# Gated DeltaNet: where e^g meets the queries, in the feature-major q or in the token rows of q S

## The chip, the cores and the metric

The kernel runs on one core of a Trainium2 chip. The metric is the device time of one execution in microseconds; times are medians over several executions. One further execution was recorded by the hardware profiler, and all lines of the profile are from it. TensorE (PE, its weight loads PEld), VectorE (DVE), ScalarE (ACT), GpSimd (POOL) and SyncE (SP, which issues most DMAs here) each work off a queue of their own, in order.

## The reference, cut to what matters

Two layers of a diffusion trunk over 128 context tokens and 256 latent tokens of 1024 features. Layer 0 runs HGRN2 and gated DeltaNet side by side between one input and one output projection; layer 1 is neighbourhood attention; each layer ends with a squared-ReLU MLP. DeltaNet has four heads of 128, goes over the tokens forward and backward, and is defined chunk by chunk:

```python
g = jnp.cumsum(glog.reshape(b, h, n, CHUNK), axis=-1)
...
attn = jnp.where(tri, jnp.einsum('bhntd,bhnsd->bhnts', q, k) * L, 0.0)
qg = q * jnp.exp(g)[..., None]
...
v_new = u_n - jnp.einsum('bhtd,bhdv->bhtv', w_n, s)
o_n = jnp.einsum('bhtd,bhdv->bhtv', qg_n, s) + jnp.einsum('bhts,bhsv->bhtv', attn_n, v_new)
s = jnp.exp(gl_n)[..., None, None] * s + jnp.einsum('bhsd,bhsv->bhdv', kdec_n, v_new)
...
o_b = _rmsnorm(ob_f + ob_b, gn_b) * jax.nn.silu(_heads(g_b, H_B).astype(f32))
```

The output of a token is the part that comes from the past, (q e^g) S, plus the part from its own chunk, attn v_new, summed over both directions and normalized. e^g is one number for each token, head and direction.

## The kernel before, in words

The 384 tokens are three tiles of 128: tile 0 is the context, tiles 1 and 2 the latents. A chunk is a whole tile here, so each tile and direction has one step of the recurrence (`gdn_step`). Tile 0 starts from no state; for tiles 1 and 2 there are the given states S0 and one state S that each direction hands on. fp32 operands of the large projections are split into two reduced-precision parts and take three matmuls (L646 to L648 for features in rows, L673 to L675 for tokens in rows); DeltaNet's own products are plain fp32, each of which the trace records as two rows.

`gdn_steps` is a generator that gives one step of DeltaNet at each "d" in the order string `STEPS`; the other letters are HGRN2's steps, the adaptive-norm products, the blocks of the input projection, the four gate blocks "g" and HGRN2's part of the output ("m"). What is written in this order is then put into each engine's queue by the framework's scheduler, which works with a simulation of its own, so that a change at one place can move instructions of other steps. `ORDER` fixes a few places by hand: the matmuls of gate 2 are held behind the last product of `gdn_out(2, ...)`, those of gate 3 behind `gdn_out(1, ...)`.

At the end of the mixer the steps around the change are these. `gdn_attn` makes k·q for all tiles (L1012) and DVE multiplies it with the decay that is already in `AT_` (L1014). `gdn_eps` squares q on ACT (L1022) and sums the squares with one-column matmuls against ones (L1024), for the epsilon of the output's norm; DVE finishes it (L1026). `gdn_qg`, for one tile and direction, makes e^g spread over features: DVE multiplies a triangle with the upper and lower part of log g (L1035), two fp32r matmuls with ones sum over tokens (L1037), ACT takes the exponential out of the bank (L1039), and POOL multiplies it into q, which lies features by tokens (L1040). `gdn_out` sums attention times new values (L1197) and this q times S (L1200) for both directions in one PSUM bank; `out_norm` squares it by head on ACT, with the sums as a second output (L1251), DVE adds epsilon (L1253), POOL takes the root (L526), and DVE scales (L1257). Tile 0 has no past and so no L1200.

Then `gdn_step` for tile 0: k S and the solved new values (L1165), the evacuation of w (L1168 on ACT), k transposed (L1173, evacuated by L1175), its product with the weighted new values (L1180) and the new state (L1183, L1186). The gate blocks run the sigmoid on ACT (L1240) and a product on DVE (L1241). `mix_out` transposes each normalized tile (L1266), multiplies the gate in and splits it (L1268 to L1271); the output projection follows.

PSUM banks rotate by tag: the tag "gd" has two banks, which each call of `ps` takes in turn, so a step that takes a bank waits until the one before the last has been read out. The pool `g2` has three buffers. L209 on ACT and L210 on DVE split a weight tile into its two parts.

Of the kernel before, what the change touches and what calls it, by code (L numbers as in the profile page):

```python
# [9 lines left out]
F32 = mybir.dt.float32  # L10
F32R = mybir.dt.float32r
AF = mybir.ActivationFunctionType
ALU = mybir.AluOpType
# [4 lines left out]
P = 128  # L18
D = 1024
KT = 8  # L20
NT = 3
# [85 lines left out]
class Trunk:  # L107
# [117 lines left out]
    def start(self):  # L225
        nc, i = self.nc, self.i
        ident, tri = self.const([P, P], "ident"), self.mixc([P, len(CONST_NAMES) - 1, P], "tri")
        self.c = {n: tri[:, k - 1] if k else ident for k, n in enumerate(CONST_NAMES)}
        nc.sync.dma_start(ident, i["consts"][:, 0, :])
        self.ones = self.mixc([P, P], "ones", F32R)  # L230
        nc.gpsimd.memset(self.ones.bitcast(F32), 1.0)
        self.c["ones"] = self.ones.bitcast(F32)
        crow = self.g2([16, P])
        nc.scalar.dma_start(crow[0:8], i["c_ctx"].rearrange("(r c) -> r c", c=P))
        nc.scalar.dma_start(crow[8:16], i["c"].rearrange("o (r c) -> (o r) c", c=P))
        brow = self.brow = self.g2([P, P])
        prow = self.prow = self.g2([76, P])
        lv = self.mixc([P, NS * 32 + 2 * P], "lv", mybir.dt.uint8)
        self.lv = {L: lv[:, k * 32:k * 32 + 32] if k < NS else lv[:, NS * 32 + (k - NS) * P:NS * 32 + (k - NS + 1) * P]
                   for k, L in enumerate(LEVELS)}  # L240
        self.eye = self.mixc([P, 32], "eye")

        def load():
            yield nc.sync.dma_start(brow[0:96], i["ada_b"].rearrange("l (r c) -> (l r) c", c=P))
            yield nc.sync.dma_start(brow[96:P], i["norm_g"].rearrange("l j (r c) -> (l j r) c", c=P))
            yield nc.sync.dma_start(prow[0:12], i["hgrn_lb"].rearrange("l (r c) -> (l r) c", c=P))
            yield nc.sync.dma_start(prow[12:13], i["gn_hgrn"])
            yield nc.sync.dma_start(prow[13:14], i["gn_gdn"])
            for j in range(2):
                yield nc.sync.dma_start(prow[14:15, j * 64:(j + 1) * 64], i["qn_na"])  # L250
                yield nc.sync.dma_start(prow[15:16, j * 64:(j + 1) * 64], i["kn_na"])
            yield nc.sync.dma_start(prow[16:76], i["gdn_conv"].rearrange("e t o (r c) -> (e t o r) c", c=P))

        def load_masks():
            nc.sync.dma_start(tri, i["consts"][:, 1:, :])
            nc.sync.dma_start(self.eye, i["levels"][:, 0:32])
            f = self.sb([P, NS * 32 + 2 * P], "lvf")
            nc.sync.dma_start(f, i["levels"][:, 32:])
            nc.gpsimd.tensor_copy(lv, f)
        self.eps = self.const([P, 5], "eps")  # L260
        nc.vector.memset(self.eps[:, 0:1], EPS)
        nc.vector.memset(self.eps[:, 1:2], EPS * P)
        nc.vector.memset(self.eps[:, 2:3], 1.0)
        nc.vector.memset(self.eps[:, 3:4], 0.0)
        nc.vector.memset(self.eps[:, 4:5], -0.5)
        pt = self.ps([P, 16], "tmp")
        nc.tensor.transpose(pt, crow, self.c["ident"][0:16, 0:16])
        cond = self.sb([P, 16], "sel")
        nc.vector.tensor_copy(cond, pt)
        sc = self.sb([P, 16], "sel")  # L270
        self.sigmoid(sc, cond)
        nc.vector.tensor_mul(sc, sc, cond)

        self.sc = self.const([P, 2 * KT + 30], "scz")
        nc.gpsimd.memset(self.sc, 0.0)

        self.sel = self.mixc([P, 4], "selc")
        pick = self.c["ident"].rearrange("p (g k c) -> p g k c", g=2, k=2)[:, :, :, 0:2]
        nc.vector.tensor_add(self.sel.rearrange("p (k v) -> p k v", k=2), pick[:, 0], pick[:, 1])
        nc.vector.tensor_copy(self.sc[:, 0:16].rearrange("p (k v) -> p k v", v=2), sc.rearrange("p (v k) -> p k v", v=2))  # L280
        return load, load_masks
# [428 lines left out]
    def evac_f(self, d, h):  # L710
        nc = self.nc

        def f(pg):
            s = self.cvt([P, NT, P])
            nc.scalar.activation(s, pg.rearrange("p (t c) -> p t c", t=NT), AF.Sigmoid)
            nc.vector.tensor_scalar(self.G[:, :, d, h], s, self.lb1[:, h:h + 1], self.lb[:, h:h + 1],
                                    op0=ALU.mult, op1=ALU.add)
# [12 lines left out]
    def hgrn_tile(self, t, Q, K):  # L730
# [5 lines left out]
        q = AT.rearrange("p h c -> p (h c)")  # L736
        G = self.G[:, t].rearrange("p d h c -> p d (h c)")
        nc.scalar.activation(K, G, AF.Identity, scale=-1.0, bias=self.eps[:, 2:3])
        ks = self.km([P, 512])
# [5 lines left out]
        for h, r, c in small:  # L745
            nc.tensor.matmul(pd[r, h], ks[:, c], q[:, c], start=True, stop=True)
        nc.vector.tensor_mul(Q[:, 0], q, G[:, 1])
        nc.vector.tensor_mul(Q[:, 1], q, G[:, 0])
        nc.vector.tensor_mul(AB, pd, self.eye.unsqueeze(1).broadcast_to([P, 4, 32]))
        tot, nt = G, 512  # L750
        yield
# [125 lines left out]
    def gates(self, h):  # L877

        nc, i = self.nc, self.i
# [31 lines left out]
        nc.vector.tensor_add(a, a, e)  # L911
        self.glog = c8("glog")
        nc.vector.tensor_mul(self.glog, a, al.unsqueeze(1).broadcast_to([P, NT, 8]))
        self.gparts = [self.mixc([P, NT, 8], n, F32R) for n in ("ghi", "glo")]
        nc.gpsimd.tensor_copy(self.gparts[0], self.glog)
        nc.gpsimd.tensor_tensor(self.gparts[1], self.glog, self.gparts[0].bitcast(F32), op=ALU.subtract)

        e3 = self.mixc([P, 3, NT, 8], "eg")
        self.eg, self.egd, self.egl = e3[:, 0], e3[:, 1], e3[:, 2]
        pe = self.ps([P, 3, NT, 8], "tmp")  # L920
# [95 lines left out]
    def gdn_eps(self):  # L1016
# [7 lines left out]
                nc.tensor.matmul(pq[:, t, h:h + 1], q2[:, t], self.c["ones"][:, 0:1], start=True, stop=True)  # L1024
        self.qe = self.mixc([P, NT, 4], "qe")
        nc.vector.tensor_scalar(self.qe, pq, EPS * EPS * P, None, op0=ALU.add)  # L1026

    def gdn_qg(self, t, d):

        nc = self.nc  # L1030
        tri = ("le", "ge")[d]
        pe = self.ps([P, 4, P], "gd")
        for n, g in enumerate(self.gparts):
            G = self.g2([P, 4, P], F32R)
            nc.vector.tensor_tensor(G, self.c[tri].unsqueeze(1).broadcast_to([P, 4, P]),  # L1035
                g[:, t, d * 4:d * 4 + 4].bitcast(F32).unsqueeze(2).broadcast_to([P, 4, P]), op=ALU.mult)
            nc.tensor.matmul(pe, self.ones, G, start=(n == 0), stop=(n == 1))  # L1037
        G = self.g2([P, 4, P])
        nc.scalar.activation(G, pe, AF.Exp)  # L1039
        nc.gpsimd.tensor_tensor(G, G, self.kq[:, t, :, 1], op=ALU.mult)  # L1040
        return G

    def gdn_solve(self):

# [142 lines left out]
                                               op0=ALU.mult, op1=ALU.add)  # L1187
        return w, S2

    def gdn_out(self, t, w, S):  # L1190
        nc = self.nc
        qg = [self.gdn_qg(t, d) for d in range(2)] if S is not None else None
        po = self.ps([P, 4, P], "gd")
        for h in range(4):
            for d in range(2):
                last = d == 1 and S is None
                self.mark["out", t] = nc.tensor.matmul(po[:, h], self.AT_[:, t, d, h], w[d][:, h], start=(d == 0), stop=last)  # L1197
            if S is not None:
                for d in range(2):
                    nc.tensor.matmul(po[:, h], qg[d][:, h], S[d][:, h], start=False, stop=(d == 1))  # L1200
        self.out_norm(1, t, po, self.vt[:, t])

    def gdn_steps(self):

        nc, i = self.nc, self.i
        for _ in zip(self.gdn_levels(0), self.gdn_levels(1)):
            yield
        S0 = self.sm4([P, 2, 4, P])
        nc.sync.dma_start(S0, i["state_gdn"][0, 0].rearrange("d h k v -> k d h v"))
        w, S = {}, {}  # L1210
        w[1, 0], S[0] = self.gdn_step(1, 0, S0[:, 0], True)
        yield
        w[2, 1], S[1] = self.gdn_step(2, 1, S0[:, 1], True)
        yield
        w[2, 0], _ = self.gdn_step(2, 0, S[0], False)
        yield
        w[1, 1], _ = self.gdn_step(1, 1, S[1], False)
        yield
        self.gdn_attn()
        self.gdn_eps()  # L1220
        yield
        self.gdn_out(2, (w[2, 0], w[2, 1]), (S[0], S0[:, 1]))
        yield
        self.gdn_out(1, (w[1, 0], w[1, 1]), (S0[:, 0], S[1]))
        yield
        for d in range(2):
            w[0, d], Sp = self.gdn_step(0, d, None, True)
            nc.sync.dma_start(self.o["state_gdn"][0, 0, d].rearrange("h k v -> k h v"), Sp)
            yield
        self.gdn_out(0, (w[0, 0], w[0, 1]), None)  # L1230
        yield
# [593 lines left out]
```

## Time and profile before

| | |
|---|---|
| median of 3 runs | 1148.52 us (1146.92 to 1149.19) |
| the profiled execution | 1152.35 us, span 1150.6 us |
| mean granted TensorE clock | 0.976 |
| busy: PE / DVE / ACT / POOL | 95% / 66% / 43% / 25% of the span |
| first L1024 to the first matmul of the output projection | 288.95 to 339.92 us |
| the first table load and exponential of L1039 | 1.28 and 0.60 us |

A row of the profile names the line of the kernel, the engine, the operation and the tiles, as out<-in. Waits are given as the engine and line that waited, "<-" the line that released it, then the total, the number and the longest. The granted clock is the share of full speed that TensorE's throttle allowed.

### The profile page before, as it was taken

The page shows a single profiled execution, that of the slowest core. Times are in us where ns is not written, and L with a number is a line of the kernel's source. Part 1 is how long each engine was busy: PE and PEld are TensorE (multiplying, and loading weights), DVE is VectorE, ACT ScalarE, POOL GpSimd, SP SyncE. Part 2 cuts the span into 40 slices and gives each one's busy share as a digit, 9 for nine tenths or more (in the row PEclk, how much of TensorE's full clock was granted, in tenths as well). Part 3 has the DMA queues.
Part 4 walks back from the last instruction along what each step waited for, and adds up shares of the span by engine and source line. Part 5 has one row for each costly group of instructions (what it writes and reads, how often), then busy time and mean ns, then how long its engine had stood idle before and what let it go on. Part 6 is the DMA issues. An engine that isn't in the chain of part 4 may idle for free.

```text
span 1150.6 us, 18007 instructions
## 1 busy us (share of the span) xinstructions
PE 1088.7 (95%) x6861; PEld 943.6 (82%) x6861; DVE 760.7 (66%) x1186; ACT 490.1 (43%) x874; POOL 289.9 (25%) x301
## 2 busy tenths in 40 slices
PE   6989978999899899999999989999988999999998
PEld 3868767988888888898889878888768889989987
DVE  3678598895356697986898565877757763333333
ACT  3465333333354553333343455555635433433330
POOL 0064894231222210120121334424012011101102
PEclk9989988999799899999999999999999999999999
DMA  8953624333043597775774228666524964333311
GB/s 283 292 166 112 215 97 131 114 109 126 19 129 110 176 318 274 255 245 178 238 242 161 74 55 196 192 181 158 142 74 126 331 192 138 128 114 125 110 37 56
DMA packets 142091, 184.66 MB, mean 160 GB/s; under 512 B 36803, under 2 KB 113685, under 8 KB 142005
## 3 DMA queue, kind: packets, MB, share of 16 engines
q1 hardware_dynamic: 141685, 183.44, 50.6%
q8 instruction: 54, 0.88, 0.3%
q14 instruction: 32, 0.26, 0.1%
q10 hardware_dynamic: 320, 0.07, 0.0%
HBM read 171.53 MB, written 4.61 MB: 153 GB/s over the span
## 4 chain that ended last, share of the span: by engine, by line
PE 73%; DMA 7%; POOL 7%; DVE 6%; SPq 3%; issue 2%; ACT 2%; POOLq 0%; DVEq 0%; ACTq 0%
PE acc L1344 7%; PE tmp L1359 7%; PE tmp L1360 7%; PE acc L1346 7%; PE acc L1345 7%; PE tmp L1358 7%; POOL sm L1071 2%; POOL sm L1072 2%; DMA ada<-in_ada_w 2%; PE acc L646 2%; PE acc L647 2%; PE po L1735 2%; PE acc L673 2%; PE acc L674 1%; PE acc L648 1%
## 5 line engine op out<-in xcount | busy, mean ns | idle before, releaser
L209 ACT ACTIVATE whi<-raw 128x1024 fp32r<-128x1024 f32 x198 | 205.9, 1050 | 331.3 <-PE acc L1346 212.0
L210 DVE TENSOR_TENSOR wlo<-raw,whi 128x1024 fp32r<-128x1024 f32 x192 | 237.3, 1246 | 162.7 <-ACT whi L209 159.4
L1378 POOL TENSOR_TENSOR h<-h 128x384 f32<-128x384 f32 x56 | 69.9, 1248 | 423.7 <-ACT h L1375 408.2
L1345 PE MATMUL acc<-wlo,h 128*128 128x512 f32 x380 | 148.5, 391 | 0.0
L1344 PE MATMUL acc<-whi,h 128*128 128x512 f32 x380 | 146.2, 393 | 0.1
L347 DVE SCALAR_TENSOR_TENSOR adc<-adr,scz,adc 128x1024 f32<-128x1024 f32 x98 | 127.8, 1335 | 9.4 <-DMA adr<-in_ada_w 9.2
L1346 PE MATMUL acc<-whi,h 128*128 128x512 f32 x380 | 121.1, 391 | 0.0
L1344 PEld LDWEIGHTS acc<-whi,h 128*128 128x128 f32 x380 | 71.1, 188 | 20.1 <-ACT whi L209 5.6
L1359 PE MATMUL tmp<-hyA,whi 128*128 128x384 f32 (+1 forms) x256 | 85.2, 333 | 2.1 <-DVE hyA L566 2.1
L1358 PE MATMUL tmp<-hyA,whi 128*128 128x384 f32 (+1 forms) x256 | 84.3, 335 | 1.5 <-ACT whi L209 1.5
L1360 PE MATMUL tmp<-hyA,wlo 128*128 128x384 f32 (+1 forms) x256 | 84.9, 333 | 0.0
L1358 PE MATMUL tmp<-hyB,whi 128*128 128x384 f32 (+1 forms) x256 | 83.7, 329 | 1.2 <-DVE hyB L565 1.2
L1359 PE MATMUL tmp<-hyB,whi 128*128 128x384 f32 (+1 forms) x256 | 84.1, 329 | 0.7 <-DVE hyB L566 0.7
L1345 PEld LDWEIGHTS acc<-wlo,h 128*128 128x128 f32 x380 | 71.4, 188 | 14.0 <-DVE wlo L210 0.2
L1346 PEld LDWEIGHTS acc<-whi,h 128*128 128x128 f32 x380 | 71.0, 188 | 13.7
L1360 PE MATMUL tmp<-hyB,wlo 128*128 128x384 f32 (+1 forms) x256 | 82.1, 328 | 0.0
L646 PE MATMUL acc<-hyA,whi 128*128 128x384 f32 x208 | 74.7, 359 | 0.9 <-DVE hyB L707 0.9
L647 PE MATMUL acc<-hyA,whi 128*128 128x384 f32 x208 | 72.3, 348 | 0.0
L648 PE MATMUL acc<-hyA,wlo 128*128 128x384 f32 x208 | 72.0, 347 | 0.0
L1379 DVE TENSOR_TENSOR h<-h,h 128x384 fp32r<-128x384 f32 (+2 forms) x72 | 38.5, 535 | 41.1 <-POOL h L1378 40.5
L526 POOL TENSOR_TENSOR ss<-ss,eps 128x1 f32<-128x1 f32 (+2 forms) x30 | 35.7, 1194 | 68.9 <-DVE ss L545 21.1
L1359 PEld LDWEIGHTS tmp<-hyA,whi 128*128 128x128 f32 x256 | 49.3, 193 | 3.3 <-DVE hyA L566 2.3
(458 smaller groups left out, 2402.9 us busy)
## 6 DMA issues: line engine op xcount, KB each, us to landing
raw<-in_w_mlp SPq DMA_DIRECT2D x128, 512.0 KB, 3.8
adr<-in_ada_w SPq DMA_DIRECT2D x80, 512.0 KB, 4.7
raw<-in_w_in_ab SPq DMA_DIRECT2D x34, 512.0 KB, 4.5
ada<-in_ada_w SPq DMA_DIRECT2D x32, 256.0 KB, 5.5
raw<-in_w_qkv_na SPq DMA_DIRECT2D x32, 256.0 KB, 3.1
raw<-in_w_out_ab SPq DMA_DIRECT2D x8, 512.0 KB, 4.0
m<-gs SPq DMA_DIRECT2D x8, 512.0 KB
raw<-in_w_qkv_na SPq DMA_DIRECT2D x8, 512.0 KB
```

The lines of the kernel that those rows point to most:

```text
L209: self.nc.scalar.activation(hi, x, AF.Copy)
L210: (eng or self.nc.vector).tensor_tensor(lo, x, hi.bitcast(F32), op=ALU.subtract)
L347: nc.vector.scalar_tensor_tensor(acc[v], raw, s[v], acc[v], op0=ALU.mult, op1=ALU.add)
L646: nc.tensor.matmul(pg[n], whi(k)[:, c], hhi[:, k], start=(k == 0), stop=False)
L647: nc.tensor.matmul(pg[n], whi(k)[:, c], hlo[:, k], start=False, stop=False)
L648: nc.tensor.matmul(pg[n], wlo(k)[:, c], hhi[:, k], start=False, stop=(k == KT - 1))
L1344: nc.tensor.matmul(pg, shi, w2hi(n)[:, o], start=start, stop=False)
L1345: nc.tensor.matmul(pg, shi, w2lo(n)[:, o], start=False, stop=False)
L1346: nc.tensor.matmul(pg, slo, w2hi(n)[:, o], start=False, stop=last)
L1358: nc.tensor.matmul(pg[n], w1hi(k)[:, c], hhi[:, k, tc_], start=(k == 0), stop=False)
L1359: nc.tensor.matmul(pg[n], w1hi(k)[:, c], hlo[:, k, tc_], start=False, stop=False)
L1360: nc.tensor.matmul(pg[n], w1lo(k)[:, c], hhi[:, k, tc_], start=False, stop=(k == KT - 1))
```

## The change

e^g is no longer spread over features and multiplied into q. A new function `gdn_past` multiplies the plain q with S (tokens come out as rows), and e^g is applied to the product as a column, one number per token row: for direction 0 by ACT's copy out of PSUM with the column as its scale, for direction 1 by DVE, which multiplies by the column and adds the first direction in the same instruction. The columns `eg` exist already. Both tiles' pasts are made right behind `gdn_attn`, ahead of `gdn_eps`. `gdn_out` sums only attention times new values in PSUM, DVE adds the past, and `out_norm` reads the sum from SBUF instead of PSUM. `gdn_qg` goes, and with it the two parts of log g and the fp32r ones.

```diff
-        self.ones = self.mixc([P, P], "ones", F32R)
-        nc.gpsimd.memset(self.ones.bitcast(F32), 1.0)
-        self.c["ones"] = self.ones.bitcast(F32)
+        self.c["ones"] = self.mixc([P, P], "ones")
+        nc.gpsimd.memset(self.c["ones"], 1.0)
...
-        self.gparts = [self.mixc([P, NT, 8], n, F32R) for n in ("ghi", "glo")]
-        nc.gpsimd.tensor_copy(self.gparts[0], self.glog)
-        nc.gpsimd.tensor_tensor(self.gparts[1], self.glog, self.gparts[0].bitcast(F32), op=ALU.subtract)
...
-    def gdn_qg(self, t, d):
...
-        pe = self.ps([P, 4, P], "gd")
-        for n, g in enumerate(self.gparts):
-            G = self.g2([P, 4, P], F32R)
-            nc.vector.tensor_tensor(G, self.c[tri].unsqueeze(1).broadcast_to([P, 4, P]),
-                g[:, t, d * 4:d * 4 + 4].bitcast(F32).unsqueeze(2).broadcast_to([P, 4, P]), op=ALU.mult)
-            nc.tensor.matmul(pe, self.ones, G, start=(n == 0), stop=(n == 1))
-        G = self.g2([P, 4, P])
-        nc.scalar.activation(G, pe, AF.Exp)
-        nc.gpsimd.tensor_tensor(G, G, self.kq[:, t, :, 1], op=ALU.mult)
-        return G
...
+    def gdn_past(self, t, S):
+
+        nc = self.nc
+        o = self.g2([P, 4, P])
+        for d in range(2):
+            pq = self.ps([P, 4, P], "gd")
+            for h in range(4):
+                nc.tensor.matmul(pq[:, h], self.kq[:, t, h, 1], S[d][:, h], start=True, stop=True)
+            for h in range(4):
+                eg = self.eg[:, t, d * 4 + h:d * 4 + h + 1]
+                if d:
+                    nc.vector.scalar_tensor_tensor(o[:, h], pq[:, h], eg, o[:, h], op0=ALU.mult, op1=ALU.add)
+                else:
+                    nc.scalar.activation(o[:, h], pq[:, h], AF.Copy, scale=eg)
+        return o
...
-    def gdn_out(self, t, w, S):
...
-        qg = [self.gdn_qg(t, d) for d in range(2)] if S is not None else None
+    def gdn_out(self, t, w, past):
+        nc = self.nc
         po = self.ps([P, 4, P], "gd")
         for h in range(4):
             for d in range(2):
-                last = d == 1 and S is None
-                self.mark["out", t] = nc.tensor.matmul(po[:, h], self.AT_[:, t, d, h], w[d][:, h], start=(d == 0), stop=last)
-            if S is not None:
-                for d in range(2):
-                    nc.tensor.matmul(po[:, h], qg[d][:, h], S[d][:, h], start=False, stop=(d == 1))
+                self.mark["out", t] = nc.tensor.matmul(po[:, h], self.AT_[:, t, d, h], w[d][:, h], start=(d == 0), stop=(d == 1))
+        if past is not None:
+            nc.vector.tensor_add(past, past, po)
+            po = past
         self.out_norm(1, t, po, self.vt[:, t])
...
         self.gdn_attn()
+        past = {2: self.gdn_past(2, (S[0], S0[:, 1])), 1: self.gdn_past(1, (S0[:, 0], S[1]))}
         self.gdn_eps()
         yield
-        self.gdn_out(2, (w[2, 0], w[2, 1]), (S[0], S0[:, 1]))
-        yield
-        self.gdn_out(1, (w[1, 0], w[1, 1]), (S0[:, 0], S[1]))
+        self.gdn_out(2, (w[2, 0], w[2, 1]), past[2])
+        yield
+        self.gdn_out(1, (w[1, 0], w[1, 1]), past[1])
```

Lines behind the change shift by a few: L1024 becomes L1020, L1165 L1146, L1168 L1149, L1173 L1154, L1175 L1156, L1180 L1161, L1197 L1192, L1240 L1236, L1251 L1247, L1257 L1253, L1270 L1266 and L673 L672. The new products are L1178, the copies L1184, the DVE steps L1182 and the addition L1194.

More of the change, by code (lines that the diff above doesn't have):

```diff
@@ L1026, in gdn_eps @@
         nc.vector.tensor_scalar(self.qe, pq, EPS * EPS * P, None, op0=ALU.add)
-    def gdn_qg(self, t, d):
-        nc = self.nc
-        tri = ("le", "ge")[d]
-        pe = self.ps([P, 4, P], "gd")
-        for n, g in enumerate(self.gparts):
-            G = self.g2([P, 4, P], F32R)
-            nc.vector.tensor_tensor(G, self.c[tri].unsqueeze(1).broadcast_to([P, 4, P]),
-                g[:, t, d * 4:d * 4 + 4].bitcast(F32).unsqueeze(2).broadcast_to([P, 4, P]), op=ALU.mult)
-            nc.tensor.matmul(pe, self.ones, G, start=(n == 0), stop=(n == 1))
-        G = self.g2([P, 4, P])
-        nc.scalar.activation(G, pe, AF.Exp)
-        nc.gpsimd.tensor_tensor(G, G, self.kq[:, t, :, 1], op=ALU.mult)
-        return G
     def gdn_solve(self):
```

## The prediction

> **What bounds the kernel now.** TensorE is busy 95% of the span, so only what it executes, what it waits for and the clock it is granted can move the end. I first split the stage that the diff touches, from the end of DeltaNet's attention products to the start of the output projection (columns: stretch, length, busy time of PE, PEld, DVE, ACT, POOL, granted TensorE clock, DMA share, GB/s).
>
> ```profile
> 288.90:305.20 16.30, 13.38 (x62) 11.69 (x63) 5.75 (x11) 3.00 (x4) 2.54 (x2) 0.58 0.00 1
> 305.20:330.00 24.80, 24.80 (x167) 24.51 (x166) 10.52 (x17) 15.15 (x45) 9.51 (x8) 1.00 0.20 64
> 330.00:339.70 9.70, 7.82 (x56) 7.55 (x54) 5.51 (x9) 3.98 (x13) 1.01 (x1) 0.82 0.62 201
> ```
>
> TensorE is idle 16.30 − 13.38 = 2.9 us in the first stretch and 1.9 us in the third, and in both it runs below full clock; the middle is full. The waits of TensorE between 270 and 345 us (total, times, longest) say for whom:
>
> ```profile
> PE gd L1197 <- ACT g L1039: 2.0, 1, 2.0
> PE gd L1180 <- ACT g L1175: 1.9, 1, 1.9
> PE gd L1024 <- DVE m L1014: 0.5, 1, 0.5
> PE gd L1037 <- DVE g L1035: 0.5, 1, 0.5
> PE gd L1200 <- POOL g L1040: 0.4, 1, 0.4
> ```
>
> Three of the five sit in `gdn_qg`. The chain that ended last (start, length, what) shows them in order of time:
>
> ```profile
> 288.95 3.22 PE gd L1024 x24
> 292.17 1.08 PE gd L1037 x2
> 293.32 1.28 ACT L1039
> 294.61 0.60 ACT g L1039
> ...
> 298.05 1.28 POOL g L1040
> 299.37 0.80 PE gd L1200 x2
> 300.17 0.85 PE gd L1197 x4
> ...
> 305.13 0.23 PE gd L1037
> ...
> 316.63 0.45 PE gd L1197 x4
> ...
> 335.35 1.90 PE gd L1180 x8
> 337.25 2.67 PE gd L1197 x16
> 339.92 0.24 PE acc L673
> ```
>
> The 1.28 us entry on ACT is the load of the exponential's table; the squares and the gate's sigmoid use another, so it is loaded anew. Four L1197 rows cost 0.85 us at 300 us and 0.45 us at 316 us: the same work, half the clock. When the clock fell:
>
> ```profile
> 291.00:291.50 0.50, 0.50 (x5) 0.50 (x5) 0.45 (x2) 0.00 (x0) 0.00 (x0) 0.69 0.00 0
> 291.50:304.50 13.00, 10.13 (x39) 8.44 (x39) 3.40 (x6) 2.48 (x3) 2.54 (x2) 0.50 0.01 1
> 331.80:335.20 3.40, 1.67 (x14) 1.39 (x13) 1.96 (x5) 3.37 (x13) 1.01 (x1) 1.00 0.64 173
> 335.20:339.20 4.00, 3.85 (x20) 3.86 (x20) 3.14 (x5) 0.61 (x2) 0.00 (x0) 0.57 0.86 310
> ```
>
> The clock is at half for 13.0 us, with 10.13 us of matmuls in it, and 0.57 in the 4.0 us behind the wait for L1175.
>
> **The change part by part.** On TensorE nothing is cheaper in itself but the eight L1037 matmuls that go: q S was 16 products on L1200 and is 16 products on the new L1178. What moves is where they stand. TensorE at 288.9 us, before:
>
> ```order
> L1024 MATMUL gd_2719<-ones,g_393_2735 128x1 x3
> L1037 MATMUL gd_2742<-g_395_2743,ones 128x512
> L1037 MATMUL gd_2742<-g_396_2746,ones 128x512
> L1197 MATMUL gd_2762<-sm_322_2195,m_121_754 128x128
> L1197 MATMUL gd_2762<-sm_311_2137,m_121_754 128x128
> L1037 MATMUL gd_2752<-g_399_2753,ones 128x512
> L1037 MATMUL gd_2752<-g_400_2756,ones 128x512
> L1200 MATMUL gd_2762<-sm_290_1968,g_397_2749 128x128
> ```
>
> and now, from the same place (m_103 holds k and q, m_121 the attention, sm the states and the new values):
>
> ```order
> L1178 MATMUL gd_2716<-sm_290_1964,m_103_650 128x128 x4
> L1178 MATMUL gd_2725<-sm_285_1947,m_103_650 128x128 x4
> L1178 MATMUL gd_2735<-sm_285_1947,m_103_650 128x128 x4
> L1178 MATMUL gd_2744<-sm_311_2133,m_103_650 128x128 x4
> L1020 MATMUL gd_2753<-ones,g_396_2754 128x1 x3
> L1192 MATMUL gd_2776<-sm_322_2191,m_121_750 128x128
> L1192 MATMUL gd_2776<-sm_311_2133,m_121_750 128x128
> ```
>
> The operands of the first four rows are ready when the stage opens; L1192 needs nothing of an exponential any more, and three of the four groups of one-column matmuls (L1020, once L1024) go in between the gate's matmuls. Now term by term.
>
> *The eight L1037 matmuls.* One at full clock is 0.23 us (305.13 us in the chain): 8 × 0.23 = 1.9 us, all on TensorE. **−1.9.**
>
> *The waits ahead of 305 us.* The idle time of the first stretch is the three waits 2.0 + 0.5 + 0.4 = 2.9 us, for the table load with the exponential, for the DVE products L1035 and for POOL's L1040. All of those steps go. **−2.9.** (The 0.5 us for L1014 lie just ahead of the stretch; L1178 now stands behind L1014 in place of L1024, and I leave that wait as it is.)
>
> *The half clock.* 10.13 us of matmul time at half clock is 5.07 us at full; with the 0.5 us at 0.69 it is about **−5.4** (it overlaps the first term a little: two pairs of L1037 ran at half clock, and only their full-clock time is counted there). I take it as saved, because the dense part of the same work at 305 to 330 us keeps 1.00.
>
> The Trainium skill ("TensorE: Matmul & The Clock Gate", Part 1, What's actually happening) puts half rate behind at least one idle window of about 3.4 us. This trace disagrees: the clock fell at 291 us, with TensorE busy on every row of L1024, and no wait in the stretch is over 2.0 us. By the page these 5.4 us would not be lost now, nor come back with shorter waits, and the sum would be 5.6 us; by the trace, they are lost to a stretch of light or half-filled work.
>
> *The tail.* ACT's queue at 332 us, before (L1168 and L1175 evacuate the step of tile 0, L1251 squares, L209 splits a weight, L1240 is the gate's sigmoid):
>
> ```order
> L1168 ACTIVATE sm_429_2888<-gd_2883 128x512
> L1251 ACTIVATE hyB_651,ss_456_3019<-hg_3006 128x128 x4
> L209 ACTIVATE whi_3408<-raw_3402 128x1024
> L1240 ACTIVATE cv_3346<-acc_3294 128x384
> L1175 ACTIVATE g_431_2895<-gd_2890 128x512
> ```
>
> and now (the same steps are L1149, L1247, L209, L1236 and L1156):
>
> ```order
> L1149 ACTIVATE sm_419_2868<-gd_2863 128x512
> L1156 ACTIVATE g_421_2875<-gd_2870 128x512
> L1247 ACTIVATE hyB_647,ss_446_2999<-hg_2986 128x128 x4
> L209 ACTIVATE whi_3388<-raw_3382 128x1024
> L1266 ACTIVATE hyB_3162<-g_476_3171 128x4x128
> L1236 ACTIVATE cv_3326<-acc_3274 128x384
> ```
>
> The evacuation for which TensorE waited 1.9 us stands now ahead of the squares, the split and the sigmoid. If nothing else is late, 1.9 us of wait and 4.0 × (1 − 0.57) = 1.7 us of clock go: 3.6. But the projection's weights arrive just there, at a DMA share of 0.86 after 335 us, and need not come the whole 12 us earlier. Bounds 0 and 3.6; I take two thirds or a little more, **−2.6**, since the loads are released by the splits that move forward with the gates.
>
> *The new evacuations.* TensorE gets a wait that it did not have: each L1178 group of tile 2 fills one of two banks, and the next tile's groups want these banks back. Prices from the nearest rows:
>
> ```profile
> L1186 DVE SCALAR_TENSOR_TENSOR sm<-sm,eg,gd x8: 328/334/342, 257.6 to 271.1; 128x128 f32<-128x128 f32 x8
> ```
>
> This is the DVE form with a column of e^g and a PSUM operand: 4 × 0.334 = 1.34 us. For ACT's copy with a column as scale, the near rows are a square out of PSUM and a copy with two columns:
>
> ```profile
> L1251 ACT ACTIVATE hyB<-gd 128x128 f32<-128x128 f32 x8 | 2.1, 278 | 8.5 <-PE gd L1200 8.5
> ```
> ```profile
> L561 ACT ACTIVATE km<-tmp,B,A x12: 436/452/459, 366.9 to 391.0; 128x128 f32<-128x128 f32 x12
> ```
>
> With one column I take the middle, 0.365, so 1.46 us for four. A group of four products is 8 rows, 0.90 us (twice the 0.45 at 316.63). Group 1 ends at 0.9, its copies at 2.4; group 2 ends at 1.8, its DVE steps, which add to the copies and so start at 2.4, at 3.8. Group 3 waits from 1.8 to 2.4 (0.6), group 4 from 3.3 to 3.85 (0.5). The one-column matmuls and the products L1192 then find their banks free, or wait some tenths for L1018's squares; I add 0.7 for these and for the second bank of the attention, which the second group takes over. **+1.8**, bounds 1.2 (copies at 278, no more waits) and 2.9 (copies at 452, and twice the rest).
>
> *Hidden.* The two DVE additions of 128x512 (0.69 us each, like L1257 on the same shape) and the two tiles' later squares stand behind `gdn_out` of tiles 2 and 1, ahead of 96 gate matmuls; nobody waits for them before the projection. Their cover is the middle stretch, in which DVE is busy 10.52 of 24.80 us. The queue of SP is ordered alike until the next layer; the two POOL operations on `gparts` ran beside TensorE at about 60 us and cost nothing.
>
> ```profile
> L1257 DVE TENSOR_TENSOR hyB<-gd,ss 128x512 f32<-128x512 f32 x2 | 1.4, 692 | 3.8 <-POOL ss L526 3.8
> ```
>
> Sum: −1.9 − 2.9 − 5.4 − 2.6 + 1.8 = −11.0 us. The profiled execution took 1152.35 us, 1.75 of it around the span, so it becomes 1141.4; it is 3.8 us above the median of 1148.52, and as the edit is an absolute saving the median becomes 1137.5.
>
> **The rivals.** *The clock stays low.* It fell under matmuls of one column, and these stay; the stretch with L1178 is full only to 3.6 of some 4.7 us. The window 331.8 to 335.2 was half filled (1.67 of 3.40 us) and a drop of the clock followed. If the light work is what counts, the 5.4 us stay and the saving is 5.6: 1142.9. Against it: three of the four one-column groups now lie among gate matmuls. Chance 0.16.
>
> *The time goes to the next layer.* The scheduler's order also changes in the attention of layer 1: SP's transfers of the weights and of the keys swap places. The queue of SP there, before, and the one wait of TensorE for it between 640 and 900 us:
>
> ```profile
> 748.32 1.58 SPq L1614 DMA_DIRECT2D raw<-in_w_qkv_na  x3
> 750.00 6.10 SPq L1645 DMA_DIRECT2D ks<-qk  x8
> ```
> ```profile
> PE sc L1700 <- DMA ks<-qk: 1.4, 1, 1.4
> ```
>
> Now the eight key transfers of this quarter go ahead of the weights, so the weights start 6.1 us later. If TensorE eats that once, the saving shrinks to 4.9: 1143.6, chance 0.08. *Slower:* if it eats it in two quarters (12.2 us) and the clock drops behind each wait, at 1.7 us each as in the tail, that is 15.6 − 11.0 = 4.6 us more: 1153.1. It decides from a loss of 11.0 us. Against it, only 1.4 us are waited for today and the weights are split ahead of use. Chance 0.04.
>
> *The stage's end doesn't move.* If the projection's weights, or the sigmoid on ACT, set its start by themselves, the gates only finish sooner and some 1 us is left: 1147.5, chance 0.03. For it speaks the DMA share of 0.86; against it the share of 0.20 from 305 to 330 us, which leaves room for those loads.
>
> **How the numbers follow.** The forecast has 0.69. Its own range runs from 1135.9 (1.2 of new waits and the full tail: −12.6) to 1141.2 (2.9, no tail: −7.3). Below I go to 1133.0, as the median before itself lies 1.6 us above its lowest run and shorter waits could lift other dips of the clock; above to 1143.5, which takes in the low clock and leaves out the rest. The times are told apart at about 0.2%, 2.3 us: the forecast, the low clock and one quarter's loss are all faster (0.93), the unmoved end is the same (0.03), two quarters' loss is slower (0.04).
>
> **What would show it right or wrong.** Right: no table load between 285 and 320 us; granted clock 1.00 from 289 us to the gates; TensorE waits on L1178 of about 0.5 us each for the copies and the DVE steps; no wait on L1161 (once L1180); the projection's first L672 at about 328.7 us (339.7 − 11.0), and the layers behind it unchanged in length. Wrong: a clock of 0.5 behind the one-column matmuls; a wait on weights ahead of L672; copies above 0.45 us; or TensorE idle for over 3 us more in the attention of layer 1 than now.

## The result and the profile after

| | before | changed |
|---|---|---|
| median | 1148.48 us (4 runs) | 1136.28 us (4 runs), ratio 0.9895, 95% interval 0.9866 to 0.9924 |
| profiled execution, span | 1152.35, 1150.6 us | 1139.19, 1137.3 us |
| mean granted clock | 0.976 | 0.983 |

The change saves 12.2 us, where 11.0 were forecast. Where they come from shows when each program is cut at two points that both have: the end of the attention's products (L1012, now L1008) and the first matmul of the output projection (L673, now L672). The windows of the kernel before (stretch, length, busy time of PE, PEld, DVE, ACT, POOL, clock, DMA share, GB/s):

```profile
0.00:288.37 288.37, 257.05 (x2345) 213.56 (x2345) 212.96 (x373) 117.97 (x213) 117.10 (x144) 0.95 0.52 164
288.37:339.68 51.31, 46.10 (x284) 43.76 (x282) 22.31 (x38) 22.13 (x62) 13.06 (x11) 0.83 0.21 69
339.68:1150.57 810.89, 785.54 (x4239) 686.31 (x4237) 525.45 (x776) 349.97 (x599) 159.76 (x146) 0.99 0.53 165
```

and of the changed kernel:

```profile
0.00:283.33 283.33, 256.06 (x2345) 212.01 (x2345) 211.76 (x373) 116.48 (x210) 115.54 (x142) 0.96 0.53 167
283.33:322.58 39.25, 37.87 (x274) 36.84 (x274) 19.25 (x37) 18.27 (x65) 8.00 (x7) 1.00 0.23 75
322.58:1137.29 814.71, 787.76 (x4239) 688.94 (x4237) 531.25 (x780) 350.37 (x599) 153.62 (x146) 0.99 0.52 165
```

The stage between the cuts is 51.31 − 39.25 = 12.06 us shorter. TensorE's idle time in it falls from 5.21 to 1.38 us, its busy time from 46.10 to 37.87 us, and the granted clock, 0.83 before, is 1.00. The 5.0 us that the changed kernel leads by ahead of the stage, and the 3.8 us that it loses behind it, are another matter: the first experiment shows them to be chance. TensorE's waits in the stage of the changed kernel are these three:

```profile
PE gd L1178 <- DVE m L1010: 0.5, 1, 0.5
PE gd L1020 <- ACT g L1018: 0.4, 1, 0.4
PE gd L1192 <- DVE qe L1022: 0.3, 1, 0.3
```

The first stood there before, for L1024. The exponential's chain and the wait for the transposed k are gone. The list names no wait of L1178 for the new evacuations, but they show in TensorE's weight loads, eight for each group of four products:

```profile
283.88 0.97 PEld L1178 LDWEIGHTS gd<-sm,m 128*128 128x128 f32 x8 [0.52 <-PE tmp L488]
285.07 0.97 PEld L1178 LDWEIGHTS gd<-sm,m 128*128 128x128 f32 x8 [0.23 <-PE gd L1178]
286.26 0.97 PEld L1178 LDWEIGHTS gd<-sm,m 128*128 128x128 f32 x8 [0.23 <-ACT g L1184]
287.52 0.97 PEld L1178 LDWEIGHTS gd<-sm,m 128*128 128x128 f32 x8 [0.28 <-DVE g L1182]
```

The groups start some 1.2 us apart, the third behind ACT's copies and the fourth behind DVE's steps. TensorE's timeline merges the 32 rows into one piece of 4.77 us, although at the rate of L1192 in the chain below (12 rows in 1.34 us) they would take 3.57: these 1.2 us are waits that the list above nearly all counts as busy time. At the stage's end, in the chain that ended last, the product that had waited (L1180, now L1161) runs at 0.89 us for its eight rows, where it took 1.90, and the projection follows at once:

```profile
320.15 1.34 PE gd L1192 x12
321.49 0.89 PE gd L1161 x8
322.38 0.45 PE gd L1192 x4
322.83 0.24 PE acc L672
```

The new evacuations, on ACT and on DVE (minimum, median and maximum in ns, then the first and the last start):

```profile
L1184 ACT ACTIVATE g<-gd,eg x8: 359/368/378, 285.1 to 288.3; 128x128 f32<-128x128 f32 x8
```
```profile
L1182 DVE SCALAR_TENSOR_TENSOR g<-gd,eg,g x8: 343/343/351, 286.3 to 289.6; 128x128 f32<-128x128 f32 x8
```

Each takes about as long as the prediction had it (0.365 and 0.334 us), but neighbours overlap: in the timeline four of them occupy their engine for little more than 1.1 us, not 1.46 and 1.34:

```profile
285.07 1.14 ACT L1184 ACTIVATE g<-gd,eg 128x128 f32<-128x128 f32 x4 [5.80 <-PE gd L1178]
...
286.34 1.13 DVE L1182 SCALAR_TENSOR_TENSOR g<-gd,eg,g 128x128 f32<-128x128 f32 x4 [1.09 <-PE gd L1178]
```

### The profile page after: what moved, and what is told of

Its sections match the earlier page's. It is cut to its first block, busy times and chain, and to the rows that moved or that the text cites. A ratio compares the mean times of both kernels' runs of the same rounds, so it can differ in the third digit from the quotient of the medians.

```text
span 1137.3 us, 17975 instructions
## 1 busy us (share of the span) xinstructions
PE 1081.7 (95%) x6853; PEld 937.8 (82%) x6853; DVE 762.3 (67%) x1188; ACT 485.1 (43%) x874; POOL 277.2 (24%) x295
## 4 chain that ended last, share of the span: by engine, by line
PE 74%; DVE 7%; DMA 6%; POOL 6%; issue 2%; SPq 2%; ACT 2%; POOLq 0%; DVEq 0%; ACTq 0%
PE acc L1340 7%; PE acc L1341 7%; PE acc L1342 7%; PE tmp L1355 7%; PE tmp L1356 7%; PE tmp L1354 7%; POOL sm L1053 2%; POOL sm L1052 2%; PE po L1731 2%; DMA ada<-in_ada_w 2%; PE acc L646 2%; PE acc L645 2%; PE acc L647 1%; PE acc L672 1%; PE acc L673 1%
## 5 line engine op out<-in xcount | busy, mean ns | idle before, releaser
L1354 PEld LDWEIGHTS tmp<-hyA,whi 128*128 128x128 f32 x256 | 48.7, 191 | 4.4 <-ACT km L560 3.4
L1355 PEld LDWEIGHTS tmp<-hyA,whi 128*128 128x128 f32 x256 | 49.3, 192 | 3.3 <-DVE hyA L565 2.4
```

The lines of the kernel that those rows point to most:

```text
L1354: nc.tensor.matmul(pg[n], w1hi(k)[:, c], hhi[:, k, tc_], start=(k == 0), stop=False)
L1355: nc.tensor.matmul(pg[n], w1hi(k)[:, c], hlo[:, k, tc_], start=False, stop=False)
```

## The experiments

The theory to test: the gain is TensorE's waits for the exponential's chain, and the clock that fell around them and behind the one-column matmuls. Its rivals: it is the work that is gone; it is the early place of q S; the clock falls with waits alone.

### Both kernels once more

No edit, a second profile of each.

> The changed kernel once more, for a second profile. In the first pair of profiles the changed kernel reached its first q S product 5.05 us earlier than the kernel before reached L1024, although TensorE's order is the same up to there. Theory: this lead is chance (half-clock windows of 3.41 us fall differently in each execution), so the start of L1178 lies elsewhere, anywhere from 282 to 290 us, while the stage from it to the first matmul of the output projection is 38 to 40 us again (38.9 in the first profile, 51.0 in the kernel before). Rival: the lead belongs to the change (the two POOL operations on log g are gone), then L1178 starts within 0.5 us of 283.9 again. Time against the kernel before: -10 to -14 us by the theory.

> The kernel before once more, for a second profile. Its profiled execution lay 3.8 us above the median, and two profiles of the changed kernel differ by 4.0 us up to the end of the attention's products. Theory: the stage from there to the output projection's first matmul is 51 us again to within 3.4 us (four to five windows of 3.41 us at half clock in it, one more or less with the phase), and what is left over lies upstream and downstream by chance. Rival: the long half-clock stretch of 13.65 us was an accident of that one execution, and the stage is 46 us or less.

The changed kernel took 1139.70 us against 1148.08 (ratio 0.9917, 0.9897 to 0.9937); the kernel before took 1147.17 against another series of itself at 1149.17 (0.9991, 0.9975 to 1.0008). The same three windows of the changed kernel:

```profile
0.00:287.33 287.33, 259.32 (x2345) 215.86 (x2345) 212.51 (x373) 116.53 (x210) 115.18 (x142) 0.95 0.52 165
287.33:326.57 39.24, 37.86 (x274) 36.83 (x274) 19.25 (x37) 18.24 (x65) 7.99 (x7) 1.00 0.23 74
326.57:1137.24 810.67, 786.19 (x4239) 687.56 (x4237) 531.85 (x780) 350.20 (x599) 153.20 (x146) 0.99 0.53 166
```

and of the kernel before:

```profile
0.00:284.81 284.81, 257.27 (x2345) 213.68 (x2345) 213.79 (x373) 117.76 (x213) 118.06 (x144) 0.95 0.52 166
284.81:336.12 51.31, 46.11 (x282) 43.77 (x282) 22.32 (x38) 22.10 (x62) 13.06 (x11) 0.83 0.22 69
336.12:1147.61 811.49, 784.25 (x4239) 686.15 (x4237) 529.03 (x776) 349.89 (x599) 153.17 (x146) 0.99 0.53 165
```

The stage repeats to 0.01 us, 51.31 and 39.24. The way to it differs by 4.0 us between the two executions of the changed kernel and by 3.6 us between those of the kernel before, in either direction between the kernels, and the way behind it by 4.0 us in the changed kernel too. So the 12.06 us of the stage belong to the change, and the rest is scatter; this is the likely reason, not a shown one, why one comparison gives 12.2 and the other 8.4 us. The rival on the POOL operations falls, as does the one on an accidental stretch of half clock.

### The arithmetic of before, made early

```diff
-        qg = [self.gdn_qg(t, d) for d in range(2)] if S is not None else None
+        qg = [self.XT[:, t, d] for d in range(2)] if S is not None else None
...
-        nc.scalar.activation(G, pe, AF.Exp)
-        nc.gpsimd.tensor_tensor(G, G, self.kq[:, t, :, 1], op=ALU.mult)
+        nc.scalar.activation(self.XT[:, t, d], pe, AF.Exp)
...
         w[2, 0], _ = self.gdn_step(2, 0, S[0], False)
+        for d in range(2):
+            self.gdn_qg(2, d)
         yield
         w[1, 1], _ = self.gdn_step(1, 1, S[1], False)
+        for d in range(2):
+            self.gdn_qg(1, d)
         yield
+        for t in (2, 1):
+            for d in range(2):
+                nc.gpsimd.tensor_tensor(self.XT[:, t, d], self.XT[:, t, d], self.kq[:, t, :, 1], op=ALU.mult)
         self.gdn_attn()
```

> The kernel before with its arithmetic kept: q e^g is still spread by two fp32r matmuls, an exponential and POOL's product, but the spreading is made one or two steps earlier, into the solved matrix's tile that is free by then, so that only plain products are left in the stage. Theory (waits and half clock are the gain, not the fewer instructions): it gets the first stretch's 2.9 us of waits and about 5 us of half clock, and keeps the 1.9 us of L1037 and the tail: 6 to 9 us below the kernel before, and no half-clock window between the attention's products and the gates. Rival (what counts is the work that is gone): no more than 2 us below.

1138.72 us against 1148.08, ratio 0.9919 (0.9891 to 0.9947): 9.4 us, as much as the changed kernel beside it. From the end of the attention's products to the projection:

```profile
289.81:327.72 37.91, 37.33 (x281) 37.25 (x281) 18.07 (x32) 17.26 (x63) 8.68 (x8) 1.00 0.26 85
```

All DVE, ACT and POOL work of e^g is still done, and the eight matmuls too; it only no longer stands in TensorE's way. No half clock is left, and 0.58 us of idle time. The rival that counts the removed work falls: it allowed 2 us. The gain is a little over the expected 6 to 9 us, and the expectation was wrong in one point: the tail's wait of 1.9 us, which it left in place, is gone as well. The clock stays at 1.00 although one-column rows still open the stage, behind the same kind of wait (0.58 us); the run with the epsilon first, below, comes back to this:

```profile
290.39 2.14 PE gd L1024 x18
```

### The new arithmetic, made late

```diff
-        past = {2: self.gdn_past(2, (S[0], S0[:, 1])), 1: self.gdn_past(1, (S0[:, 0], S[1]))}
         self.gdn_eps()
         yield
-        self.gdn_out(2, (w[2, 0], w[2, 1]), past[2])
+        self.gdn_out(2, (w[2, 0], w[2, 1]), self.gdn_past(2, (S[0], S0[:, 1])))
         yield
-        self.gdn_out(1, (w[1, 0], w[1, 1]), past[1])
+        self.gdn_out(1, (w[1, 0], w[1, 1]), self.gdn_past(1, (S0[:, 0], S[1])))
```

> The changed arithmetic, but q S made directly ahead of each tile's attention product instead of ahead of gdn_eps. Theory (the gain comes from the chain of the exponential that is gone, and from the clock that no longer drops): the place is worth little, because the new products need nothing that is late; the stage is 39 to 42 us and the time 9 to 12 us below the kernel before. It would be nearer 42 if the nine one-column matmuls that now open the stage cost one half-clock window (1.7 us). Rival (the early place is what hides the work): the copies and the addition stand on the path of both tiles, 1.5 to 2 us for each, and the clock drops again: stage 45 us or more, time less than 6 us below.

1139.02 us against 1148.08, ratio 0.9924 (0.9901 to 0.9948). The stage:

```profile
285.23:326.58 41.35, 40.63 (x283) 40.43 (x282) 21.00 (x40) 17.05 (x69) 8.09 (x7) 0.92 0.22 72
```

41.35 us is inside the theory's 39 to 42. The waits are even shorter (0.72 us idle), but the clock is 0.92. The early place is worth the 2.1 us of clock in the profile, and nothing that the times tell. With the run before, either remedy alone, a late chain without an exponential or an early one with it, brings the gain.

### Is it waits or light work that throttles the clock?

Two edits. In the changed kernel, the epsilon's one-column matmuls go first:

```diff
-        past = {2: self.gdn_past(2, (S[0], S0[:, 1])), 1: self.gdn_past(1, (S0[:, 0], S[1]))}
         self.gdn_eps()
+        past = {2: self.gdn_past(2, (S[0], S0[:, 1])), 1: self.gdn_past(1, (S0[:, 0], S[1]))}
```

> The changed kernel with two lines in the other order: gdn_eps ahead of gdn_past. TensorE's waits stay below 1 us, but 18 one-column rows stand in one piece ahead of the first q S product. Theory (one-column matmuls count as idle for the clock): one or two windows of 3.41 us at half clock right behind them, stage 41 to 43 us against 39.3, time 1 to 3.5 us above the changed kernel. Rival (only waits throttle it): no half-clock window in the stage, 39 to 40 us, the same time.

In the kernel before, they go behind the product of tile 2:

```diff
         self.gdn_attn()
-        self.gdn_eps()
...
+        if t == 2:
+            self.gdn_eps()
         self.out_norm(1, t, po, self.vt[:, t])
```

> The kernel before, with the one-column matmuls of gdn_eps made behind the product of tile 2 instead of ahead of gdn_qg; nothing is removed, and TensorE's waits for the exponential's chain stay at about 2.9 us. Theory (light work throttles the clock as well as waits do): without the 24 one-column matmuls in one piece ahead of the waits, the stretch of 13.65 us at half clock shrinks to one or two windows of 3.41 us: 3 to 5 us below the kernel before. Rival (the waits alone throttle it): half clock from the first wait on, 10 us or more of it, and the time within 1.5 us of the kernel before.

With the one-column rows first, the stage grows from 39.25 to 42.97 us, with a clock of 0.88 and only 0.72 us of idle time. The clock in windows of 3.41 us:

```profile
282.30:285.71 3.41, 2.95 (x28) 2.89 (x27) 2.74 (x6) 0.52 (x1) 0.00 (x0) 1.00 0.00 0
285.71:289.12 3.41, 3.41 (x18) 3.41 (x18) 0.00 (x0) 0.40 (x2) 0.00 (x0) 0.50 0.02 5
289.12:292.53 3.41, 3.15 (x15) 3.06 (x16) 0.56 (x3) 0.74 (x3) 1.04 (x1) 0.50 0.00 0
292.53:295.95 3.42, 3.42 (x18) 3.42 (x18) 1.13 (x5) 1.14 (x4) 0.00 (x0) 0.50 0.00 0
295.95:299.36 3.41, 3.41 (x26) 3.41 (x26) 1.42 (x4) 1.00 (x7) 0.00 (x0) 1.00 0.00 0
```

TensorE is busy for 2.95 of the 3.41 us ahead of the fall. What is special there stands in TensorE's timeline:

```profile
284.16 2.55 PE L1020 MATMUL gd<-ones,g 128*128 128x1 f32 x18 [0.46 <-DVE m L1010]
286.57 2.06 PE L1178 MATMUL gd<-sm,m 128*128 128x128 f32 x8
288.42 1.28 PE L1020 MATMUL gd<-ones,g 128*128 128x1 f32 x6
289.96 5.49 PE L1178 MATMUL gd<-sm,m 128*128 128x128 f32 x24 [0.26 <-DVE qe L1022]
```

a wait of 0.46 us and, from 284.16 to the fall at 285.71 us, 1.55 us of one-column rows. TensorE fills the second window to the last, yet the third is still at half clock: 1.70 us of the second are one-column rows. Full clock comes back behind the fourth, which is the first without any. In the changed kernel the window at the same place, 281.89 to 285.30 us, holds no more matmul time (2.89 us) and the same wait, but 128-column products behind it, and full clock follows. So the rival falls that one-column rows do not matter. They are not enough by themselves, though. In the run of the early arithmetic, the windows of 3.41 us (counted on from its earlier half-clock stretches) put the wait into one window and the one-column rows into the next: 287.05 to 290.46 us holds 1.26 us of idle time, 290.46 to 293.88 us is wholly busy with 2.14 us of one-column rows in it, and neither is followed by half clock. At waits of this size it took both in one window, and where the windows fall differs from one execution to the next. The stage is at the upper end of what was expected, with three half-clock windows for one or two, but the time did not follow, against the expectation of 1 to 3.5 us more: 1138.62 us against 1149.17 (0.9912, 0.9894 to 0.9930), no different from the changed kernel. In this profile the rest behind the stage took 808.3 us, 2.4 us less than in the second profile of the changed kernel: that one has three windows at half clock from 366.01 us on, the first profile two from 363.81 us, and this one none there. Why they are missing stays open, and so does whether other executions lose the stage's 3.7 us at all.

In the kernel before with the rows moved back, the stage is 51.34 us, as before:

```profile
287.51:338.85 51.34, 43.62 (x281) 40.89 (x281) 20.91 (x34) 22.05 (x64) 13.04 (x11) 0.93 0.20 61
```

The clock is better, 0.93 for 0.83, and the busy time 2.5 us less; but the idle time grew by as much, from 5.21 to 7.72 us, since the one-column rows had covered part of the exponential's chain and tile 1 now waits for it as well:

```profile
PE gd L1180 <- ACT g L1175: 1.9, 1, 1.9
PE gd L1197 <- ACT g L1039: 1.8, 2, 1.2
PE gd L1037 <- DVE g L1035: 1.0, 1, 1.0
PE gd L1024 <- ACT g L1022: 0.9, 1, 0.9
PE gd L1200 <- POOL g L1040: 0.7, 1, 0.7
```

More waits went with less half clock, two windows for four in a row and one in the tail. But waits of this size are enough by themselves: the second of the two windows follows 3.41 us (310.81 to 314.22 us) with 1.49 us of matmuls and no one-column row. So the expectation was right about the clock and wrong about the time. It was 1151.65 us against 1148.08, ratio 1.0026 (1.0011 to 1.0040); the 3 us more are not in the stage, and this profile does not show where they are.

### The table load alone

In the kernel before, a 128x1 exponential (of zero times a ready value, so 1.0, multiplied into the epsilon term) draws the table load forward:

```diff
         pq = self.ps([P, NT, 4], "gd")
+        one = self.sb([P, 4], "ss4")[:, 0:1]
+        nc.scalar.activation(one, self.AT_[:, 2, 0, 3, 0:1], AF.Exp, scale=0.0)
...
-        nc.vector.tensor_scalar(self.qe, pq, EPS * EPS * P, None, op0=ALU.add)
+        nc.vector.tensor_scalar(self.qe, pq, one, EPS * EPS * P, op0=ALU.mult, op1=ALU.add)
```

> The kernel before, with one 128x1 exponential of a ready value (multiplied in as 1.0 into the epsilon term) ahead of L1039, so that the exponential's table is loaded while TensorE makes the one-column matmuls. Nothing else is changed. Theory (chain and clock together): the wait for L1039 shrinks from 2.0 to 0.7 us, the half clock stays, as it sets in behind the one-column matmuls: 1 to 3 us below the kernel before. Rival (the table load is the main cost): with the longest wait gone the clock holds too, 5 us or more below.

1146.72 us against 1149.17, ratio 0.9978 (0.9963 to 0.9993). The stage and the stretch at half clock in it:

```profile
284.96:335.61 50.65, 46.72 (x283) 44.38 (x282) 22.38 (x38) 21.02 (x62) 13.05 (x11) 0.83 0.20 70
```
```profile
287.17:300.82 13.65, 12.06 (x49) 10.37 (x48) 4.33 (x7) 1.19 (x2) 2.54 (x2) 0.50 0.00 1
```

```profile
PE gd L1199 <- ACT g L1041: 0.7, 1, 0.7
```

The wait for the exponential fell from 2.0 to 0.7 us as expected, and the half clock stayed, 13.65 us of it. Only 0.66 us of the 1.3 come out of the stage: what was idle is now in part slow work. That a wait is gone does not bring the clock back.

### The tail alone

```diff
         kt = self.g2([P, 4, P])
-        nc.scalar.activation(kt, pt, AF.Copy)
+        if t:
+            nc.scalar.activation(kt, pt, AF.Copy)
+        else:
+            nc.vector.tensor_copy(kt, pt)
```

> The kernel before, with only the tail relieved: for tile 0 the transposed k is copied out of its bank by VectorE instead of ScalarE, so that it no longer stands behind the squares, the split and the sigmoid. Theory (the prediction's term for the tail): the 1.9 us wait goes and with it the 3.41 us window at half clock: 2 to 3.6 us below the kernel before. Rival (the projection's weights or the normalization hold its start anyway): within 1 us of it, with a wait of TensorE of another name in the last 8 us of the stage.

1145.19 us against 1149.17, ratio 0.9969 (0.9955 to 0.9983). The stage, and its last 8 us:

```profile
286.47:334.04 47.57, 43.79 (x290) 41.39 (x290) 22.64 (x39) 22.30 (x68) 13.05 (x11) 0.89 0.19 62
```
```profile
326.00:334.00 8.00, 7.55 (x66) 7.13 (x65) 5.30 (x9) 4.73 (x20) 1.01 (x1) 1.00 0.50 166
```

The stage is 3.74 us shorter than 51.31: the wait and the half clock of the last 8 us are gone (0.45 us idle, clock 1.00). The first stretch has less half clock in this execution too, 10.24 us for 13.65, so not all of the 3.74 need be the tail's; nor need the 4.0 us between the medians, since the kernel before had 1147.17 in its other series, only 2.0 us more. The projection's weights did not hold its start back. The normalization did a little, as the rival had it, with a wait of another name:

```profile
PE hg L1269 <- DVE hyB L1260: 0.5, 1, 0.5
```

## Why the prediction was right

*What bounds, and where the gain lies.* Right: the stage between the two cuts gives 12.06 us in both pairs of profiles, and nothing else moved beyond the scatter. The expected signs are there: no wait on the exponential or on L1161, clock 1.00. The forecast waits of about 0.5 us on L1178 for the copies and the DVE steps stand only in the weight loads, at 0.23 and 0.28 us. The start of the projection, 322.58 and 326.57 us for a forecast 328.7, was put on an absolute scale that scatters by 4 us. It is in part luck that the median came within 1.2 us of the forecast 1137.5: the second series of the changed kernel had 1139.70.

*Waits ahead of 305 us, −2.9, and the tail's wait.* The three waits went, and the tail's 1.9 with them. The idle time fell by 3.83 us, which is these 2.9 + 1.9 less new idle time of some 0.9 us.

*New evacuations, +1.8.* This held. The L1178 rows take 4.77 us for a forecast of some 4.7, 1.2 us more than in a dense stretch, and TensorE waits 0.4 and 0.3 us more behind them: 1.9 in all. The idle time alone (1.38 us less the 0.5 of L1010, which is old) would put it at 0.9. The single durations were as taken; four steps in a row overlap and occupy 0.2 to 0.3 us less, but the first copy starts 0.3 us later than in the working, so the third and the fourth group start 2.4 and 3.6 us behind the first for a forecast 2.4 and 3.85.

*Tail, −2.6 out of 3.6.* This is the term that was mis-sized: the cut for the weights' arrival was not needed. All 1.9 us of wait went, and the window of 3.41 us at half clock, 1.7 us: 3.6. The experiment on the tail alone gives 3.74, with one half-clock window less in the first stretch included.

*Half clock, −5.4.* Mechanism and size fit. The busy time fell by 8.23 us; 1.9 for L1037, 5.4 and the tail's 1.7 make 9.0, less the 1.0 us that L1178's rows are busy beyond a dense stretch (4.58 for 3.57): 8.0. The 0.2 us left over is not settled; four rows at half clock take 0.85 us and at full 0.45, which saves 47% and not half, and would add some 0.4 to it.

With the tail at 3.6 and the evacuations at 1.9 the terms sum to −11.9 for the measured −12.06. So the 11.0 was short by the tail's 1.0 us, and no large errors cancel in it.

*The rivals.* "The clock stays low" named a true mechanism: one-column matmuls beside a wait do throttle. It did not come true because the first thing behind the attention's products is now 32 rows of full width, with the one-column rows spread behind it. The prediction gave this only as a point against the rival; the run with the epsilon first shows that it can decide the clock, at 3.7 us of the stage in the one profile taken, and the run of the early arithmetic that it need not, when the wait and the one-column rows fall into different windows. The Trainium skill ("TensorE: Matmul & The Clock Gate", Part 1, What's actually happening) puts half rate behind an idle window of about 3.4 us; the windows here have that length, but the one that was followed by half clock held 2.95 us of matmuls. The rivals of layer 1 did not show: behind the stage the two kernels take 810.89 and 811.49, and 814.71 and 810.67 us.

## What to carry to other kernels

Here a chain through four engines ahead of a few matmuls cost its waits and, with one-column matmuls beside them, 13.65 us at half clock as well; it could be taken off the path by changing the arithmetic or by making it earlier, and both were worth the same. Keep one-column matmuls apart from waits, with wide ones between them; here this kept the clock in the profile, though the times did not tell it. Count what a wait costs from the length of a stretch and not from idle time alone, since the row of a merged piece can hide it. Compare a stage between two fixed instructions and repeat the profile, before a lead at some absolute time is read as an effect.

## What the runs showed of the hardware

The granted clock counts matmuls by more than their busy time: 1.55 us of one-column rows beside 0.46 us of wait, in a window of 3.41 us with 2.95 us of matmuls, came ahead of a fall to 0.50, which lasted three windows of 3.41 us, two of them wholly busy. A window with 2.89 us of matmuls and the same wait, but 128-column products for the one-column rows, was followed by full clock (the changed kernel), and so was one wholly busy with 2.14 us of one-column rows in it (the early arithmetic). One with 1.49 us of matmuls and no one-column row was followed by half clock (the kernel before with the epsilon late). How the clock weighs these is not measured. Two executions of one program, the changed kernel, differ by 4.0 us in their first 285 us, at mean clocks of 0.95 and 0.96, while a stage of 39 us repeats to 0.01 us.
